# Expert sums moved to later blocks, and the overflow branch moved into the last block, in a two-layer encoder kernel

## The chip, the cores and the metric

The kernel runs on one core of a Trainium2 chip. The metric is the device time of one execution in microseconds; the kernel before has a median of 1400.67 us over three runs (1398.75 to 1402.1).

## The reference

Two layers on 512 tokens of width 1024, all in float32. Each layer is a mixer followed by a mixture of experts:

```python
x = x + hybrid_mixer(rmsnorm(x, norm_mix[l]), ...)        # attention + short convolution, one output projection
x = x + hierarchical_moe(rmsnorm(x, norm_ffn[l]), ...)    # 32 experts, 2 per token
...
return rmsnorm(x, norm_final)
# inside hierarchical_moe, for each block of token slots of one expert e:
y = (silu(xb @ w_gate[e]) * (xb @ w_up[e])) @ w_down[e]   # 1024 -> 512 -> 1024
```

A router chooses one of four groups and two of its eight experts for each token. The outputs of the two experts are weighted and added to the token's row. Each expert has 6 MB of weights, so one layer reads about 201 MB of them.

## The kernel before, in words

**Blocks.** The tokens of all experts are packed into 14 blocks of 128 slots (`BLOCKS`, L39). The experts are ranked by load; a block holds one expert of 128 slots, two of 64, or up to four of 32. A block therefore reads 12 weight tiles of 512 KB for each of its experts: 8 for gate and up, 4 for down. Blocks 2 and 12 have four experts, block 11 three, block 4 one, the others two. The first four experts are fixed (`STATIC`), the others are read by a number that the router has put into a register.

**One block** (`block`, L1223) runs on TensorE in written order (pinned): gate and up products in four quarters of the width (banks A, 64 to 128 matmul instructions), then a SiLU on ScalarE and a product on VectorE, four transposes, a copy, and the down products (banks C). Its result is weighted and split into a high and a low part (`yhi`, `ylo`, two places of the pool t4), with a 0/1 matrix `gm` (a place of the pool t2) that says which token each slot belongs to. The functions in `btw` are called between these steps, at quarter 0 to 3, behind the SiLU and product (`"a"`), behind the transposes (`"t"`) and ahead of the down products (`"y"`).

**Sums.** `combine(b, t)` (L1269) adds block b's result to token tile t: four matmuls into the banks D and F, which have one buffer each, and two additions on VectorE into x. Before, block 2 does the sums of blocks 0 and 1, block 3 those of block 2, and every later block those of the block before it, one token tile at a time. The last block does block 12's sums at quarter 0, at quarter 1, at "a" and at "t". Its own are done by `finish`, which begins some token tiles with x itself through an identity matmul (`begin`, L1280, two tiles in layer 0 and three in layer 1, called at "y").

**Gathers.** For the first three blocks the token rows are gathered straight from x (`gather1`); for the later ones from a high and a low part of x that block 2 writes (`parts`, `all_parts`), one or two blocks ahead (`gather`, four steps, banks B with two buffers). `rows_of` and `slots` bring each slot's token number, scale and gate; they need a table that VectorE makes in block 0.

**Loads.** All weight tiles of the kernel stand in one list in the order of use. SP issues them in that order, and the program asks for the next whenever a tile has been used:

```python
def pump(most=10 ** 6):
    while most and todo and mem["held"] < N4 - mem["keep"] and todo[-1][3] <= mem["routed"]:
```

The pool t4 has 42 places (`N4`); `mem["keep"]` of them are kept for results, gathered rows, one-hot matrices and the parts of x. It is 8 from block 1, 17 from the middle of block 2 (`KEEP_PARTS`), 15 from block 3 (`KEEP_MOE`), 21 in block 12 and 28 in the mixer (`KEEP_MIX`). The next layer's mixer weights stand behind the experts in the same list. A load also waits until the place it gets is really free.

**Overflow.** If an expert has more tokens than its slots, `spill` (L1046) does the rest in a loop under a condition (L1055). With these inputs the condition is false, and each engine only passes the branch. It stands ahead of block 13, with the last three down tiles of that block behind it in SP's order.

VectorE, ScalarE and GpSimdE are put in order by a planner in the expert blocks; TensorE and SP follow the program. L173 is the wrapper through which pinned instructions are recorded, so most of TensorE's rows carry that line.

Of the kernel before, what the change touches and what calls it, by code (L numbers as in the profile page):

```python
# [20 lines left out]
NT = S // P  # L21
ND = D // P
DEPTH = 2
# [45 lines left out]
GROUPS = [(0, 1), (2,), (3, 4), (5, 6), (7, 8), (9, 10), (11, 12), (13,)]  # L69
GROUP_OF = {b: j for j, g in enumerate(GROUPS) for b in g}  # L70
WHOLE = 3
MAXB = 32
NROW = 3 + 2 * E

# [84 lines left out]
R_ATT, R_CNV, R_W, R_F, R_L = 0, 4, 8, 20, 28  # L159
N4 = 42  # L160
N2 = 6
KEEP_MIX, KEEP_OUT, KEEP_ROUTE, KEEP_FIRST, KEEP_SECOND, KEEP_PARTS, KEEP_MOE = 28, 27, 5, 6, 8, 17, 15


class Engine:
# [11 lines left out]
def trunk(ctx, tc, x_d, norm_mix, w_in, attn_sink, conv_w, norm_attn_out, norm_conv_out, w_out,  # L177
# [25 lines left out]

    todo = []
    live = {}
    mem = {"held": 0, "keep": KEEP_MIX, "routed": -1}
    expert_of = {}

    def rows(w, n):
# [43 lines left out]

    perm = {}

    def pump(most=10 ** 6):
        while most and todo and mem["held"] < N4 - mem["keep"] and todo[-1][3] <= mem["routed"]:
            key, shape, src, _ = todo.pop()
            if isinstance(src, tuple):
                w, l, o, k0, k1 = src  # L260
                if o < STATIC:
                    src = w[l, o][k0:k1]
                else:
                    src = w[l][bass.ds(expert(l, o), 1), k0:k1, :].rearrange("o p f -> (o p) f")
                if len(shape) == 3:
                    src = src.rearrange("(p i) c -> p i c", i=2)
            t = t4(shape)
            nc.sync.dma_start(t, src)
            live[key] = t
            mem["held"] += 1  # L270
            most -= 1
# [652 lines left out]
    def order(l, q):  # L924

        kc, kr = q["kc"], q["kr"]
        a0 = _cols["rank"][0]
        sc = small("sc", [E, 8])
        V.tensor_copy(sc[:, 0:1], kc[:E, 0:1])
        above = small("above", [E, E], BF16)  # L930
        V.tensor_scalar(above, kr[:E], sc[:, 0:1], None, op0=OP.is_lt)
        rp = ps("B", (P, E))
        T.matmul(rp, onesb[:E], above, start=True, stop=True)

        mt = small("mt", [E, E])
        V.tensor_scalar(mt, rp[:E], cst[:E, a0:a0 + 1], None, op0=OP.is_equal)
        pf = small("pf", [E, E])
        V.tensor_tensor(pf, mt, iota[:E, :E], op=OP.mult)
        V.tensor_reduce(sc[:, 1:2], pf, axis=AX.X, op=OP.add)
        pm = small("perm", [E, 1], I32, bufs=2)  # L940
        V.tensor_copy(pm, sc[:, 1:2])
        perm[l] = pm
        mem["routed"] = l
        q.update(sc=sc, mt=mt)
# [189 lines left out]
    def moe(l, before):  # L1134
# [4 lines left out]
        def onehot(j):  # L1139

            b, w = GROUPS[j][0], len(GROUPS[j]) * P
            sq = small("sq", [P, 2, NT], bufs=2)
            GP.tensor_scalar(sq, q["v"][:, 16:18, :], -float(b * P), None, op0=OP.add)
            oh = t4([P, NT, 2 * P], F32R)
            io = iota[:, :w]
            for t in range(NT):
                V.tensor_scalar(oh[:, t, :w], io, sq[:, 0, t:t + 1], None, op0=OP.is_equal)  # L1147
                V.scalar_tensor_tensor(oh[:, t, :w], io, sq[:, 1, t:t + 1], f(oh[:, t, :w]), op0=OP.is_equal, op1=OP.add)
            ohq[j] = oh

        def gather1(b, c0, c1):

            if c0 == 0:
                hg[b] = t4([P, ND, P])
            j = GROUP_OF[b]
            s = (b - GROUPS[j][0]) * P
            for c in range(c0, c1, 2):
                p = ps("B", (P, 2, P))
                for cc in range(2):
                    for t in range(NT):  # L1160
                        T.matmul(p[:, cc], chunk(t, c + cc), f(ohq[j][:, t, s:s + P]), start=t == 0, stop=t == NT - 1)
                for cc in range(2):
                    A.activation(hg[b][:, c + cc], p[:, cc], AF.Copy, scale=g_ffn[:, c + cc:c + cc + 1])
# [37 lines left out]
        def rows_of(j):  # L1201
            w = len(GROUPS[j]) * P
            p = ps("B", (P, 2 * P))
            for t in range(NT):
                T.matmul(p[:NROW, :w], st["tab"][:, t], ohq[j][:, t, :w], start=t == 0, stop=t == NT - 1)
            st["rows"] = t2([NROW, 2 * P])
            A.activation(st["rows"][:, :w], p[:NROW, :w], AF.Copy)

        def slots(j):

            m = len(GROUPS[j])
            p = ps("B", (P, 2, 2 + E))
            for n in range(m):
                T.matmul(p[:, n], st["rows"][:, n * P:(n + 1) * P], C("sel")[:NROW], start=True, stop=True)
            g = small("tg", [P, 2, 3], bufs=4)
            V.tensor_copy(g[:, :m, :2], p[:, :m, :2])
            for n, b in enumerate(GROUPS[j]):
                tg[b] = g[:, n]
                for o in range(FIRST[b], FIRST[b] + len(BLOCKS[b])):
                    for s, w in tiles_of(OFF[o], SLOTS[o]):  # L1220
                        V.tensor_copy(g[s:s + w, n, 2:3], p[s:s + w, n, 2 + o:3 + o])
# [47 lines left out]
        def combine(b, t, tags="DF"):  # L1269
            yhi, ylo, gm = yy[b]  # L1270
            for n in range(2):
                s = slice(n * 512, (n + 1) * 512)
                p = ps(tags[n])
                T.matmul(p, gm[:, t * P:(t + 1) * P], yhi[:, s], start=True, stop=False)
                T.matmul(p, gm[:, t * P:(t + 1) * P], ylo[:, s], start=False, stop=True)
                V.tensor_add(x[:, t, s], x[:, t, s], p)  # L1276
# [3 lines left out]
        def begin(t):  # L1280

            sums[t] = [ps(tag) for tag in BANKS[l][t]]
            for n in range(2):
                T.matmul(sums[t][n], ident, x[:, t, n * 512:(n + 1) * 512], start=True, stop=False)
# [24 lines left out]

        def first():  # L1310

            rows_of(0)
            gather1(1, 0, 2)
            slots(0)

        def both(*what):
            return lambda: [fn() for fn in what]
# [6 lines left out]
        for b in range(NBLK):  # L1324
            if b == 5:
                nbb = past(q)
            if b == 6:
                et, ni = places(q, nbb)
            if b == 8:
                over = et, nc.values_load(  # L1330
                    ni[0:1, 0:1], min_val=0, max_val=MAXB,
                    skip_runtime_bounds_check_because="an expert's slots are 32 at least: fewer blocks than experts")
            c = [lambda t=t: combine(b - 1, t) for t in range(NT)]
            j = GROUP_OF[b] + 1
            if b == 0:
                btw = {0: lambda: order(l, q), 1: rest, 3: first, "a": lambda: gather1(1, 2, ND)}
            elif b == 1:
                mem["keep"] = KEEP_SECOND
                btw = {1: lambda: onehot(1), "a": both(lambda: rows_of(1), lambda: gather1(2, 0, 4)),
                       "t": both(lambda: slots(1), lambda: gather1(2, 4, ND))}  # L1340
            elif b == 2:
                c = [lambda t=t: (combine(0, t), combine(1, t)) for t in range(NT)]
                ga = [lambda k=k: gather(j, k) for k in range(0, ND, 2)]
                btw = {1: lambda: onehot(j), 2: all_parts, "a": both(lambda: rows_of(j), ga[0], c[0], ga[1], c[1]),
                       "t": both(ga[2], c[2], lambda: slots(j), ga[3], c[3])}
            elif b == NBLK - 1:
                btw = {0: c[0], 1: c[1], "a": c[2], "t": c[3]}
            elif b % 2:
                mem["keep"] = KEEP_MOE
                ga = [lambda k=k: gather(j, k) for k in (0, 2)]  # L1350
                btw = {1: lambda: onehot(j), "a": both(c[0], ga[0], c[1]), "t": both(c[2], ga[1], c[3])}
            else:
                ga = [lambda k=k: gather(j, k) for k in (4, 6)]
                btw = {"a": both(lambda: rows_of(j), c[0], ga[0], c[1]), "t": both(c[2], lambda: slots(j), ga[1], c[3])}
            pin(*((T,) if b < PIN_MOE else ()))
            if b == NBLK - 2:
                mem["keep"] = KEEP_MOE + 6
            if b == NBLK - 1:
                mem["keep"] = KEEP_MIX if l < DEPTH - 1 else KEEP_MOE
                if overflow:  # L1360
                    spill(l, q, *over)
                btw["y"] = lambda: [begin(t) for t in range(AHEAD[l])]
            block(b, btw)
        pin()
        return lambda t: finish(t) if l == DEPTH - 1 or t < AHEAD[l] else combine(NBLK - 1, t, BANKS[l][t])

    def nothing(t):
# [49 lines left out]
```

## Time and profile before

| | |
|---|---|
| runs, median (lowest to highest) | 1400.67 us (1398.75 to 1402.1) |
| profiled execution, its own time | 1399.71 us |
| its span, granted TensorE clock | 1397.9 us, 0.996 |
| TensorE busy | 1334.8 us (95%) |
| VectorE, ScalarE, GpSimdE busy | 607.0, 374.5, 118.9 us |
| read from HBM | 436 MB, 313 GB/s on the mean |

The span runs from the first to the last instruction; the execution's own time is 1.8 us more. The expert blocks of layer 0 run from about 230 to 697 us and those of layer 1 from about 921 to 1385 us. A busy TensorE is not one at its peak, because the ends of matmuls are modelled; what it waited for is in the views of waits.

### The profile page before, as it was taken

The page shows a single profiled execution, that of the slowest core. Times are in us where ns is not written, and L with a number is a line of the kernel's source. Part 1 is how long each engine was busy: PE and PEld are TensorE (multiplying, and loading weights), DVE is VectorE, ACT ScalarE, POOL GpSimd, SP SyncE. Part 2 cuts the span into 40 slices and gives each one's busy share as a digit, 9 for nine tenths or more (in the row PEclk, how much of TensorE's full clock was granted, in tenths as well). Part 3 has the DMA queues.
Part 4 walks back from the last instruction along what each step waited for, and adds up shares of the span by engine and source line. Part 5 has one row for each costly group of instructions (what it writes and reads, how often), then busy time and mean ns, then how long its engine had stood idle before and what let it go on. Part 6 is the DMA issues. An engine that isn't in the chain of part 4 may idle for free. (4 is left out here: it accounts for less than half of the span.)

```text
span 1397.9 us, 21902 instructions
## 1 busy us (share of the span) xinstructions
PE 1334.8 (95%) x7783; PEld 774.0 (55%) x7783; DVE 607.0 (43%) x1483; ACT 374.5 (27%) x816; POOL 118.9 (9%) x130
## 2 busy tenths in 40 slices
PE   5999999999999999999989999999999999999897
PEld 4888786545554444433368887865445444454143
DVE  4788845224244322312267888451442332333032
ACT  4556631221111111101155666222211111111012
POOL 2101440000000000000040014300000000000000
PEclk9999999999999999999999999999999999999999
DMA  8521368899999999999881224698999999999995
GB/s 268 170 76 61 116 247 300 347 375 355 419 385 390 419 418 419 418 419 419 331 265 46 76 63 149 256 342 334 382 383 418 360 418 419 418 419 419 419 418 222
DMA packets 161106, 439.61 MB, mean 314 GB/s; under 512 B 19368, under 2 KB 56416, under 8 KB 160992
## 3 DMA queue, kind: packets, MB, share of 16 engines
q1 hardware_dynamic: 160992, 438.16, 81.1%
q8 instruction: 63, 1.03, 0.3%
q14 instruction: 51, 0.42, 0.1%
HBM read 436.00 MB, written 2.10 MB: 313 GB/s over the span
## 5 line engine op out<-in xcount | busy, mean ns | idle before, releaser
L173 PE MATMUL A<-t,t 128*32 128x512 f32 (+3 forms) x3724 | 719.2, 526 | 16.9 <-DMA t<-in_w_expert_gate_dram 4.2
L173 PEld LDWEIGHTS A<-t,t 128*32 128x32 f32 (+2 forms) x3724 | 343.1, 144 | 351.0 <-issue 232.0
L173 PE MATMUL C<-t,t 128*32 128x512 f32 (+4 forms) x1384 | 233.6, 568 | 3.1 <-DMA t<-in_w_expert_down_dram 1.6
L173 PEld LDWEIGHTS C<-t,t 128*32 128x32 f32 (+2 forms) x1384 | 84.6, 128 | 136.8 <-issue 112.9
L390 DVE SCALAR_TENSOR_TENSOR t<-C,tg,t 128x512 fp32r<-128x512 f32 x56 | 41.5, 749 | 202.5 <-ACT t L389 200.7
L1245 DVE SCALAR_TENSOR_TENSOR t<-A,tg,t 128x512 f32<-128x512 f32 x28 | 21.0, 751 | 237.2 <-PE A L173 233.6
L173 PE MATMUL B<-t,t 128*128 128x256 f32 (+3 forms) x836 | 113.4, 285 | 7.2 <-DVE t L1170 4.7
L173 PEld LDWEIGHTS B<-t,t 128*128 128x128 f32 (+1 forms) x836 | 105.0, 188 | 24.3 <-DVE t L1170 7.6
L1276 DVE TENSOR_TENSOR x<-x,D 128x512 f32<-128x512 f32 x104 | 71.1, 684 | 92.0 <-PE D L173 91.6
L173 PE MATMUL D<-t,t 128*128 128x512 f32 (+1 forms) x374 | 99.8, 366 | 5.7 <-DVE t L387 2.9
L1244 ACT ACTIVATE t<-A,tg 128x512 f32<-128x512 f32 x28 | 19.2, 687 | 319.0 <-PE A L173 319.0
L389 ACT ACTIVATE t<-C,tg 128x512 fp32r<-128x512 f32 x56 | 37.8, 686 | 208.6 <-PE C L173 208.4
L173 POOL TENSOR_TENSOR t<-t,t 128x512 f32<-128x512 f32 (+1 forms) x34 | 63.8, 1880 | 234.0 <-PE A L173 122.1
L173 PE MATMUL B<-cst,t 128*128 128x128 f32 (+1 forms) x396 | 60.7, 281 | 20.2 <-DVE t L173 19.0
L1185 ACT ACTIVATE t<-B,gf 128x256 f32<-128x256 f32 (+1 forms) x96 | 38.6, 454 | 144.4 <-PE B L173 138.0
L173 PEld LDWEIGHTS D<-t,t 128*128 128x128 f32 x374 | 53.8, 179 | 32.5 <-issue 8.1
L173 PE MATMUL F<-t,t 128*128 128x512 f32 x214 | 71.3, 413 | 0.2
L1276 DVE TENSOR_TENSOR x<-x,F 128x512 f32<-128x512 f32 x104 | 70.7, 680 | 0.3 <-PE F L173 0.3
L173 PEld LDWEIGHTS B<-cst,t 128*128 128x128 f32 (+1 forms) x396 | 49.8, 153 | 32.3 <-issue 11.1
L173 PEld LDWEIGHTS F<-t,t 128*128 128x128 f32 x214 | 38.2, 190 | 17.1 <-DVE x L1276 9.1
L386 ACT ACTIVATE t<-t 128x1024 fp32r<-128x1024 f32 x44 | 46.1, 1057 | 0.2
L1147 DVE TENSOR_SCALAR t<-cst,sq 128x256 fp32r<-128x256 f32 (+1 forms) x64 | 17.2, 332 | 65.2 <-PE A L173 53.3
(250 smaller groups left out, 1019.1 us busy)
## 6 DMA issues: line engine op xcount, KB each, us to landing
t<-in_w_expert_gate_dram SPq DMA_DIRECT2D x256, 512.0 KB, 9.8
t<-in_w_expert_up_dram SPq DMA_DIRECT2D x256, 512.0 KB, 9.8
t<-in_w_expert_down_dram SPq DMA_DIRECT2D x256, 512.0 KB, 9.8
t<-in_w_in_dram SPq DMA_DIRECT2D x36, 512.0 KB, 6.3
t<-in_w_out_dram SPq DMA_DIRECT2D x16, 512.0 KB, 3.6
x<-in_x_dram SPq DMA_DIRECT2D x4, 512.0 KB
out_dram<-t SPq DMA_DIRECT2D x3, 512.0 KB, 2.6
t<-in_norm_mix_dram SPq DMA_DIRECT2D x2, 512.0 KB
```

Of the source, the lines that this page charges most:

```text
L173: return (lambda *args, **kw: self.tc.keep_in_program_order(fn(*args, **kw))) if self.pinned else fn
L386: A.activation(hi, src, AF.Copy)
L389: A.activation(hi, src, AF.Copy, scale=scale)
L390: V.scalar_tensor_tensor(lo, src, scale, f(hi), op0=OP.mult, op1=OP.subtract)
L1147: V.tensor_scalar(oh[:, t, :w], io, sq[:, 0, t:t + 1], None, op0=OP.is_equal)
L1185: A.activation(hg[b][c // 4][:, c % 4 + cc, :w], p[:, cc, :w], AF.Copy, scale=g_ffn[:, c + cc:c + cc + 1])
L1244: A.activation(a, pg, AF.Silu, scale=rs)
L1245: V.scalar_tensor_tensor(a, pu, rs, a, op0=OP.mult, op1=OP.mult)
L1276: V.tensor_add(x[:, t, s], x[:, t, s], p)
```

## The change

Block 0's sums are done in block 3, those of blocks 1 and 2 in block 4, those of 3 and 4 in block 5, and from block 6 on each block does those of the block before it, as it did. The last block does all four token tiles' sums of block 12 at quarters 0 and 1. The overflow branch moves from ahead of block 13 into it, to "a"; `begin` is called at "t". The places kept are 18 from block 2 and 20 in blocks 3 and 4; the last block keeps 15, and the mixer's tiles alone still obey 28 (`room`). In block 0 the first gather steps are called ahead of `rows_of` and `slots`.

```diff
+SUMS = {3: [0], 4: [1, 2], 5: [3, 4]}
...
-KEEP_PARTS, KEEP_MOE = 17, 15
+KEEP_PARTS, KEEP_LATE, KEEP_MOE = 18, 20, 15
...
+    def room(key):
+        return max(mem["keep"], KEEP_MIX) if key[0] in ("gm", "in", "rope", "mask", "out") and mem["experts"] else mem["keep"]
...
         def first():
+            gather1(1, 0, 2)
             rows_of(0)
-            gather1(1, 0, 2)
+            gather1(1, 2, 4)
             slots(0)
...
-            c = [lambda t=t: combine(b - 1, t) for t in range(NT)]
+            late = SUMS.get(b, [b - 1])
+            c = [lambda t=t: [combine(n, t) for n in late] for t in range(NT)]
...
             elif b == 2:
-                c = [lambda t=t: (combine(0, t), combine(1, t)) for t in range(NT)]
                 ga = [lambda k=k: gather(j, k) for k in range(0, ND, 2)]
-                btw = {1: lambda: onehot(j), 2: all_parts, "a": both(lambda: rows_of(j), ga[0], c[0], ga[1], c[1]),
-                       "t": both(ga[2], c[2], lambda: slots(j), ga[3], c[3])}
+                btw = {1: lambda: onehot(j), 2: all_parts, "a": both(lambda: rows_of(j), ga[0], ga[1]),
+                       "t": both(ga[2], lambda: slots(j), ga[3])}
             elif b == NBLK - 1:
-                btw = {0: c[0], 1: c[1], "a": c[2], "t": c[3]}
+                mem["keep"] = KEEP_MOE
+                btw = {0: both(c[0], c[1]), 1: both(c[2], c[3]), "a": lambda: spill(l, q, *over),
+                       "t": lambda: [begin(t) for t in range(AHEAD[l])]}
             elif b % 2:
-                mem["keep"] = KEEP_MOE
+                mem["keep"] = KEEP_LATE if b == 3 else KEEP_MOE
...
-            if b == NBLK - 1:
-                mem["keep"] = KEEP_MIX if l < DEPTH - 1 else KEEP_MOE
-                if overflow:
-                    spill(l, q, *over)
-                btw["y"] = lambda: [begin(t) for t in range(AHEAD[l])]
             block(b, btw)
```

## Rows read from the trace of the kernel before

**Rows 1.** Stretches of layer 0: length, busy time by engine, clock, DMA share, GB/s.

```profile
293.70:339.30 45.60, 42.33 (x302) 22.39 (x300) 20.92 (x36) 10.61 (x17) 0.23 (x1) 0.93 0.92 359
...
394.00:442.00 48.00, 48.00 (x295) 20.16 (x293) 17.42 (x47) 6.29 (x11) 0.23 (x1) 1.00 0.98 374
442.00:600.00 158.00, 158.00 (x1116) 76.64 (x1112) 53.47 (x113) 24.68 (x48) 0.23 (x1) 1.00 1.03 418
...
680.00:692.00 12.00, 11.74 (x44) 4.74 (x42) 3.53 (x6) 0.60 (x1) 0.00 (x0) 1.00 0.54 191
```

**Rows 2.** Waits of TensorE, 229.7 to 600 us: total, times, longest.

```profile
PE B L173 <- DVE t L1199: 1.2, 1, 1.2
```

**Rows 3.** Waits of TensorE, 600 to 660 us.

```profile
PE A L173 <- DMA t<-in_w_expert_gate_dram: 2.1, 9, 0.5
```

**Rows 4.** Waits of the SP queue in block 2, 293.7 to 339.3 us.

```profile
SPq L268 <- PE B L173: 9.0, 2, 8.6
```

**Rows 5.** Waits of the SP queue, 394 to 442 us.

```profile
SPq L268 <- PE A L173: 9.7, 11, 2.7
SPq L268 <- PE F L173: 6.2, 1, 6.2
```

**Rows 6.** Timeline of TensorE in block 2 of layer 1: start, us, instruction.

```profile
1004.03 0.63 PE L173 MATMUL D<-t,t 128*128 128x512 f32 x2
...
1005.45 0.73 PE L173 MATMUL D<-t,t 128*128 128x512 f32 x2 [0.32 <-DVE x L1276]
...
1006.61 2.07 PE L173 MATMUL B<-t,t 128*128 128x256 f32 x16
```

**Rows 7.** Costliest groups of the page: the gathers' evacuation.

```profile
L1185 ACT ACTIVATE t<-B,gf 128x256 f32<-128x256 f32 (+1 forms) x96 | 38.6, 454 | 144.4 <-PE B L173 138.0
```

**Rows 8.** Timeline of TensorE in blocks 3 and 4 of layer 1.

```profile
1028.05 13.95 PE L173 MATMUL A<-t,t 128*64 128x512 f32 x64
...
1071.70 0.63 PE L173 MATMUL D<-t,t 128*128 128x512 f32 x2
...
1072.62 2.08 PE L173 MATMUL B<-t,t 128*128 128x256 f32 x16
```

**Rows 9.** Timeline of TensorE in block 0 of layer 0.

```profile
246.08 0.69 PE L173 MATMUL B<-t,t 128*67 128x256 f32 x4 [1.24 <-DVE t L1199]
```

**Rows 10.** Timeline of TensorE in the last block, layers 0 and 1.

```profile
661.79 4.21 PE L173 MATMUL A<-t,t 128*64 128x512 f32 x16 [0.82 <-ACTq L1055]
...
681.49 0.73 PE L173 MATMUL D<-t,t 128*128 128x512 f32 x2
...
682.52 0.61 PE L173 MATMUL B<-cst,t 128*128 128x128 f32 x4
...
684.66 1.12 PE L173 MATMUL D<-x,cst 128*128 128x512 f32 x2 [0.26 <-DVE x L1276]
...
688.29 6.26 PE L173 MATMUL C<-t,t 128*64 128x512 f32 x26
694.78 1.93 PE L173 MATMUL C<-t,t 128*64 128x512 f32 x6 [0.23 <-DMA t<-in_w_expert_down_dram]
...
1377.91 7.09 PE L173 MATMUL C<-t,t 128*64 128x512 f32 x32
```

**Rows 11.** The branch's line, layer 0: count, ns, first and last start.

```profile
L1055 SPq EVENT_SEMAPHORE  x9: 17/17/17, 676.6 to 686.3; - x9
L1055 PEldq COMPARE_BRANCH  x1: 353/353/353, 659.1 to 659.1; - x1
L1055 PEldq EVENT_SEMAPHORE  x1: 51/51/51, 661.0 to 661.0; - x1
...
L1055 SPq COMPARE_BRANCH  x1: 50/50/50, 676.4 to 676.4; - x1
```

**Rows 12.** Timeline of the SP queue at the end of layer 0.

```profile
676.03 11.82 SPq L268 DMA_DIRECT2D t<-in_w_expert_down_dram  x3
...
693.33 28.85 SPq L268 DMA_DIRECT2D t<-in_w_in_dram  x17
```

More of the change, by code (lines that the diff above doesn't have):

```diff
@@ L161 @@
 N2 = 6
-KEEP_MIX, KEEP_OUT, KEEP_ROUTE, KEEP_FIRST, KEEP_SECOND, KEEP_PARTS, KEEP_MOE = 28, 27, 5, 6, 8, 17, 15
+KEEP_MIX, KEEP_OUT, KEEP_ROUTE, KEEP_FIRST, KEEP_SECOND, KEEP_PARTS, KEEP_LATE, KEEP_MOE = 28, 27, 5, 6, 8, 18, 20, 15
 class Engine:
@@ L205, in trunk @@
     live = {}
-    mem = {"held": 0, "keep": KEEP_MIX, "routed": -1}
+    mem = {"held": 0, "keep": KEEP_MIX, "routed": -1, "experts": False}
     expert_of = {}
@@ L254, in trunk @@
     perm = {}
+    def room(key):
+        return max(mem["keep"], KEEP_MIX) if key[0] in ("gm", "in", "rope", "mask", "out") and mem["experts"] else mem["keep"]
     def pump(most=10 ** 6):
-        while most and todo and mem["held"] < N4 - mem["keep"] and todo[-1][3] <= mem["routed"]:
+        while most and todo and mem["held"] < N4 - room(todo[-1][0]) and todo[-1][3] <= mem["routed"]:
             key, shape, src, _ = todo.pop()
@@ L1332, in moe @@
                     skip_runtime_bounds_check_because="an expert's slots are 32 at least: fewer blocks than experts")
-            c = [lambda t=t: combine(b - 1, t) for t in range(NT)]
+            late = SUMS.get(b, [b - 1])
+            c = [lambda t=t: [combine(n, t) for n in late] for t in range(NT)]
             j = GROUP_OF[b] + 1
             if b == 0:
-                btw = {0: lambda: order(l, q), 1: rest, 3: first, "a": lambda: gather1(1, 2, ND)}
+                mem["experts"] = True
+                btw = {0: lambda: order(l, q), 1: rest, 3: first, "a": lambda: gather1(1, 4, ND)}
             elif b == 1:
@@ L1341, in moe @@
             elif b == 2:
-                c = [lambda t=t: (combine(0, t), combine(1, t)) for t in range(NT)]
                 ga = [lambda k=k: gather(j, k) for k in range(0, ND, 2)]
-                btw = {1: lambda: onehot(j), 2: all_parts, "a": both(lambda: rows_of(j), ga[0], c[0], ga[1], c[1]),
-                       "t": both(ga[2], c[2], lambda: slots(j), ga[3], c[3])}
+                btw = {1: lambda: onehot(j), 2: all_parts, "a": both(lambda: rows_of(j), ga[0], ga[1]),
+                       "t": both(ga[2], lambda: slots(j), ga[3])}
             elif b == NBLK - 1:
-                btw = {0: c[0], 1: c[1], "a": c[2], "t": c[3]}
+                mem["keep"] = KEEP_MOE
+                btw = {0: both(c[0], c[1]), 1: both(c[2], c[3]), "a": lambda: spill(l, q, *over),
+                       "t": lambda: [begin(t) for t in range(AHEAD[l])]}
+                if not overflow:
+                    del btw["a"]
             elif b % 2:
-                mem["keep"] = KEEP_MOE
+                mem["keep"] = KEEP_LATE if b == 3 else KEEP_MOE
                 ga = [lambda k=k: gather(j, k) for k in (0, 2)]
@@ L1357, in moe @@
                 mem["keep"] = KEEP_MOE + 6
-            if b == NBLK - 1:
-                mem["keep"] = KEEP_MIX if l < DEPTH - 1 else KEEP_MOE
-                if overflow:
-                    spill(l, q, *over)
-                btw["y"] = lambda: [begin(t) for t in range(AHEAD[l])]
             block(b, btw)
         pin()
+        mem["keep"] = KEEP_MIX if l < DEPTH - 1 else KEEP_MOE
+        mem["experts"] = False
         return lambda t: finish(t) if l == DEPTH - 1 or t < AHEAD[l] else combine(NBLK - 1, t, BANKS[l][t])
```

## The prediction

> **What bounds the kernel now.** I read the page's slices first: in both layers the transfers run near 420 GB/s through most of the expert blocks and far below it in the mixers, so the expert stage is where this change can act. Then a table by stretches of layer 0 [rows 1]. Block 2 (293.7 to 339.3 us) moved 359 GB/s, blocks 5 and 6 (394 to 442) 374, and from 442 to 600 it is 418 with TensorE busy throughout. After that the waits of TensorE: up to 600 us it waits on no transfer at all, only on other engines; from 600 to 660 it waits on expert weights [rows 2, 3]. So the stage has two halves. First TensorE sets the pace and the transfers stop for lack of free buffers; then the blocks of three and four experts come, transfers set the pace, and the stage ends when the last tile has landed. A tile is 512 KB, 1.25 us at 418 GB/s.
>
> The queue that issues the loads (SP) shows what ties the halves together [rows 4, 5]: in block 2 it stood 8.6 us on one gather's matmul, in blocks 5 and 6 on TensorE's expert products (9.7 us) and 6.2 us on one sum's matmul (F). All of these are buffers given back late by TensorE. From 442 us on nothing stops it but its own pace. Therefore the end of the stage moves by what TensorE's time moves up to block 6, not by how the idle transfer time is spread before that: an early gap that is filled only runs sooner into the same limit of buffers.
>
> **The change part by part.** Layers repeat each other, so I price one and say where they differ.
>
> *Sums leave block 2.* There two sums of one token tile stand back to back. The first starts at 1004.03 and the gather behind the second at 1006.61: 2.58 us, with a 0.32 us wait for VectorE to have emptied the same bank D [rows 6]. Four pairs are 10.3 us. They also cover bank waits of the gathers: without them a gather that needs the bank of the one two places back waits for two evacuations of 0.454 us [rows 7] with only four short matmuls (about 0.5) in between, twice, 2 x 0.4 to 0.5 = about 1.0. Net -9.3 us of TensorE time in block 2; nothing is late instead, for block 3's first ten weight tiles have been issued before the gap.
>
> *Sums arrive in blocks 3, 4 and 5.* Block 3 does block 0's sums in place of block 2's, same count: 0. Blocks 4 and 5 do two blocks' sums in place of one, and again back to back on the banks D and F. A lone sum costs 0.92 us to the next matmul (1071.70 to 1072.62) [rows 8]; I take four at 4.1, since one of them follows the transposes and meets a bank not yet emptied. Four pairs are 10.3 as above. So +6.2 each, +12.4 together. This is dearer than what block 2 gives, because eight pairs now meet the busy bank where four did. Bounds: if VectorE's additions overlapped fully a pair would be 2 x 0.92 and each block +3.3; if every addition had also to wait for other VectorE work, I add half a us to a pair, +8.2.
>
> *Fewer weight tiles held* (18 places kept for other tiles in place of 17 in block 2, 20 in place of 15 in blocks 3 and 4). In block 4 the queue may be 5 tiles shorter, 6.3 us of transfer. Block 5's first 22 of 24 tiles still fit before its products begin, so TensorE does not starve: 0 on its own account. What it takes is reserve, which has to be refilled in block 5.
>
> *First block.* TensorE stood 1.24 us for the table before rows_of [rows 2, 9]; the first gather, 16 matmuls, needs only the one-hot tile and now fills it. Some of it returns as bank waits of 0.25 each between the reordered gathers. I take -1.0 (ends 0 and -1.6).
>
> TensorE's time up to block 6 is therefore -1.0 - 9.3 + 12.4 = +2.1 us a layer. In layer 0 the granted clock of block 2 is 0.93 on the mean [rows 1], and part of that stretch lies behind waits for the high and low parts of x; those waits stay, and what runs at the lower level is then the gathers in place of the sums. I leave that out of the sum and in the range. I pass the whole +2.1 on to the stream of loads. The ends: -1.3 (if transfers run without a break from block 5's products on, they are one tile ahead at 442 us) and +4.6 (the full 2.1 and two tiles late, 2 x 1.25, since block 5 now holds two blocks' results of two places each).
>
> *Last block, sums in its own waits.* Its expert products stand from 661.79 to 681.49, 19.7 us, of which 64 matmuls are 13.95, as in block 3 [rows 8], and two sums 2.2; the rest, 3.5, is waiting for weights, and 0.82 stand ahead of it for the branch [rows 10]. Two more sums and their pair waits are 2.9 us more work (two pairs of 2.58 in place of two sums) against 4.3 of waiting. Not all of the waiting lies behind them: I take the end of the products 0.4 later in layer 0 and, where the same stretch is 0.6 shorter (an estimate), 0.9 later in layer 1. Between the products and the first matmul of the next sums there were 3.17 us (681.49 to 684.66). Of these the chain product, transposes keeps 1.03 + 0.61 (681.49 to 682.52 and the transposes); the two sums and a 0.26 wait for VectorE go: -1.5. The branch joins this chain.
>
> *The branch.* Before, each engine passed it between blocks 12 and 13. SP went in at 676.4 and came out at 686.3, having waited for its loads in flight, and the last three down tiles were issued only then [rows 11, 12]; 680 to 692 us moved 191 GB/s [rows 1]. TensorE's down products started at 688.29 and ended at 694.78 + 1.93 = 696.7 where layer 1's took 7.09 without a break [rows 10]: 1.3 us lost on those tiles. Now the three are issued ahead of the branch and follow at 1.25 each, done near 687, while their products begin at 687: the 1.3 goes. In its new place the branch stands ahead of the transposes, which need VectorE to have passed it. VectorE's own passage is not in the rows; TensorE's took from 659.1 to 661.0, part of it finishing its matmuls [rows 11]. Bounds 0 and 1.9; I take 0.3, for the engines that had nothing left to finish needed only their compare (50 ns on SP). Six loads of the next layer now go out before the branch and SP waits for them too; the others follow at about 695 us (687 and six times 1.25), where before the second w_in tile and those behind it began at 693.3 [rows 12]. 0, covered by the norm and transposes that the next layer begins with.
>
> Tail: layer 0: +0.4 - 1.5 + 0.3 - 1.3 = -2.1; layer 1 has no stall on down tiles: +0.9 - 1.5 + 0.3 = -0.3.
>
> **Sum.** 2 x 2.1 - 2.1 - 0.3 = +1.8 us on the profiled execution's 1399.71 (span 1397.9 and 1.8 around it), 1401.5. That execution lies 1.0 below the median of the runs shown, 1400.67, so the median becomes 1402.5. A measurement of this kernel tells 0.2%, 2.8 us, from no change: my forecast is no change that can be told, on the slower side.
>
> **The rivals.**
>
> *The stream keeps what block 2 loses.* 45.6 us at 359 in place of 418 GB/s are 6.5 us of transfer in layer 0 [rows 1]. For it: the 8.6 us wait is SP's longest in that block, and it does go. Against it: the limit is met again by 442 us, and at block 5's products the stream now stands at 22 tiles of that block and not 27. Without any break from there it gains 1.3 a layer; with the tail at its better end (branch 0, products not late: -2.8 and -1.5) the time is 1400.67 - 2.6 - 4.3 = 1393.8; with half of that, 1397. Chance 0.24. The Trainium skill has the rule that speaks for it (Perfetto Trace Analysis, Identifying the Most-Contended Engine: take the engine with the highest use, transfers by their bandwidth, and improve that first); by it the 6.5 us of layer 0 would come back in full. No run here shows that yet; the trace shows the limit returning.
>
> *Slower: results held two blocks on starve SP in block 5.* Place: 405 to 425 us and the like in layer 1, where SP already waited 6.2 us on a sum's F matmul [rows 5]. With two blocks' results in the buffers until the last pair of block 5, that wait begins earlier and ends later. It decides once SP stands longer than the tiles in flight last, about 10 us, since the page has a load land 9.8 us after its issue. Price: two tiles more a layer, 2.1 + 2.5 each: 1400.67 + 9.2 - 2.4 = 1407.5. Chance 0.20.
>
> *Slower: the branch on the chain.* 1.9 us exposed in each layer in place of 0.3, and SP's wait for the six loads of the next layer holding the rest back: 1402.5 + 3.2 = 1405.7, more if layer 1's first products then wait. For it: it now lies on the one chain that ends each layer. Against it: TensorE's 1.9 includes the end of its matmuls, which has to be waited for anyway. Chance 0.10.
>
> **How the numbers follow.** Forecast 0.46 (1399 to 1404.5 with the stage at +1 to +3 a layer), the stream 0.24, starved SP 0.20, branch 0.10. Faster by over 0.2% (below 1397.9): nearly all of the stream's rival, 0.22, and 0.02 of the forecast's edge: 0.24. Slower by over 0.2% (above 1403.5): 0.18 of the starved queue, 0.08 of the branch, 0.05 of the forecast's upper edge: 0.31. Same 0.45. The range for 8 times in 10 is 1396 to 1408: below it is the better half of the stream's rival, above it both layers at the upper end. The forecast's own range is 1399 to 1404.5.
>
> **What would show it.** TensorE's sums gone from block 2, the next block starting some 10 us sooner; in blocks 4 and 5 four pairs of about 2.6 us, and block 6 starting about 2 us later than before. SP's 8.6 us wait on a gather gone, a longer one on a sum's F matmul in block 5; the table's rate near 418 in block 2 and lower than 374 in blocks 5 and 6. In layer 0's last block no idle transfers between 680 and 687 us and no wait of the down products; their start about 1 us sooner after the last weights. Wrong would be: block 6 starting sooner than before, a rate of 400 or more from 394 to 442, or transposes of the last block over 1 us behind the product.

## The result, and the profile after

The changed kernel took 1407.65 us on the median (1405.83 to 1408.32, 4 runs), the kernel before 1399.71 (1398.24 to 1402.1, 4 runs) on the same chip: ratio 1.0053, 95% interval 1.0038 to 1.0068. It is slower by some 7 us, more than the 0.2% that can be told from no change. The forecast was 1402.5 us and no change that can be told; slower than that had a chance of 0.31. The result lies above the forecast's own range (1399 to 1404.5), 0.35 us inside the wide one (1396 to 1408), and at the time of a rival (1407.5). The profiled execution has a span of 1406.5 us, 8.6 more than before, and granted clock 0.993 against 0.996.

Line numbers shift: L173 is now L175, L268 L274, L1055 L1061, L1170 L1176, L1276 L1282. First the stretches of layer 0 after (length, busy time by engine, clock, DMA share, GB/s), against [rows 1]:

```profile
293.70:339.30 45.60, 41.90 (x314) 19.79 (x312) 14.76 (x30) 11.56 (x19) 0.46 (x2) 0.96 1.02 407
394.00:442.00 48.00, 46.60 (x266) 20.38 (x268) 22.57 (x55) 5.49 (x10) 0.23 (x1) 1.00 0.87 329
442.00:600.00 158.00, 158.00 (x1108) 71.98 (x1100) 49.74 (x106) 23.51 (x44) 0.23 (x1) 1.00 1.03 417
680.00:692.00 12.00, 10.47 (x44) 3.84 (x40) 1.87 (x4) 1.28 (x2) 0.00 (x0) 1.00 1.03 416
```

Block 2's stretch gained 48 GB/s and 394 to 442 us lost 45, where the queue stopped. The waits of SP, first in block 2 (against [rows 4]), then from 394 to 442 us (against [rows 5]): the 8.6 us on a gather have become 2.1, the 6.2 us on a sum's F matmul 10.4.

```profile
SPq L274 <- PE B L175: 2.5, 2, 2.1
```

```profile
SPq L274 <- PE F L175: 11.8, 2, 10.4
SPq L274 <- PE A L175: 9.4, 10, 2.6
```

A pair of sums in block 4 (start, us, instruction) is 2.57 us (374.28 to 376.85) with the same 0.33 wait for VectorE as in [rows 6]:

```profile
374.28 0.63 PE L175 MATMUL D<-t,t 128*128 128x512 f32 x2
...
375.68 0.73 PE L175 MATMUL D<-t,t 128*128 128x512 f32 x2 [0.33 <-DVE x L1282]
...
376.85 2.07 PE L175 MATMUL B<-t,t 128*128 128x256 f32 x16
```

Block 2 of layer 1, without sums, shows what they had covered: waits for an evacuation (0.49) and for VectorE's slots (0.77).

```profile
1005.60 4.67 PE L175 MATMUL B<-t,t 128*128 128x256 f32 x25 [0.63 <-DVE t L1176]
1010.11 0.60 PE L175 MATMUL B<-cst,t 128*128 128x128 f32 x4
1011.20 2.18 PE L175 MATMUL B<-t,t 128*128 128x256 f32 x16 [0.49 <-ACT t L1191]
1013.21 0.53 PE L175 MATMUL B<-cst,t 67*128 67x34 f32 x4
1014.52 2.15 PE L175 MATMUL B<-t,t 128*128 128x256 f32 x16 [0.77 <-DVE tg L1227]
```

From the transposes (1010.11) to the next gather are 1.09 us, from the slots' matmuls (1013.21) to theirs 1.31. In the kernel before, with sums ahead of each, they were 0.35 and 0.37:

```profile
1011.10 0.60 PE L173 MATMUL B<-cst,t 128*128 128x128 f32 x4
1011.45 2.16 PE L173 MATMUL B<-t,t 128*128 128x256 f32 x16
...
1016.02 0.53 PE L173 MATMUL B<-cst,t 67*128 67x34 f32 x4
1016.39 2.15 PE L173 MATMUL B<-t,t 128*128 128x256 f32 x16
```

The 25 gather matmuls at 1005.60 had a granted clock of 0.67 on the mean of their stretch, so they ran largely at the lower of the two levels, 1.2 GHz:

```profile
1005.00:1010.20 5.20, 4.60 (x26) 4.61 (x27) 0.54 (x1) 0.84 (x2) 0.00 (x0) 0.67 1.03 420
```

One thing is not in the program's order: in both layers 36 of block 8's 128 products (tiles 128*32) stand among block 7's sums.

```profile
479.87 0.63 PE L175 MATMUL D<-t,t 128*128 128x512 f32 x2
480.43 1.06 PE L175 MATMUL A<-t,t 128*32 128x512 f32 x6
481.42 0.73 PE L175 MATMUL F<-t,t 128*128 128x512 f32 x2
481.99 0.60 PE L175 MATMUL B<-cst,t 128*128 128x128 f32 x4
482.51 1.90 PE L175 MATMUL A<-t,t 128*32 128x512 f32 x10
...
489.05 1.92 PE L175 MATMUL A<-t,t 128*32 128x512 f32 x14
```

The last block of layer 0, against [rows 10], and the branch's rows on VectorE, against [rows 11] (count, ns, first and last start):

```profile
668.78 1.93 PE L175 MATMUL A<-t,t 128*64 128x512 f32 x6 [0.22 <-DMA t<-in_w_expert_up_dram]
...
679.78 7.09 PE L175 MATMUL A<-t,t 128*64 128x512 f32 x32
688.39 0.63 PE L175 MATMUL B<-cst,t 128*128 128x128 f32 x4 [1.53 <-DVEq L1061]
...
692.38 7.09 PE L175 MATMUL C<-t,t 128*64 128x512 f32 x32
```

```profile
L1061 DVEq COMPARE_BRANCH  x1: 72/72/72, 687.6 to 687.6; - x1
L1061 DVEq EVENT_SEMAPHORE  x1: 21/21/21, 688.2 to 688.2; - x1
```

The down products now run without a break (7.09), and the transposes stand 1.52 behind the products' end (679.78 + 7.09 = 686.87) against 1.03 before (in layer 1 there are 1.08 after). Behind VectorE's product, which ends at 687.73, they stand 0.66, under the 1 us that the prediction names as a sign of being wrong; behind TensorE's products it was over 1 us before, too.

Taken from the timelines at each boundary, the 8.6 us of span come out so (changed less before, us):

| stretch | forecast a layer | layer 0 | layer 1 |
|---|---|---|---|
| ahead of block 0: first mixer; second mixer | 0 | +1.24 | +0.64 |
| block 0 | -1.0 | -0.74 | -0.74 |
| block 2 | -9.3 | -9.2 | -7.1 |
| blocks 4 and 5 | +12.4 | +12.9 | +12.9 |
| start of block 0 to start of block 6 (sum) | +2.1 | +2.96 | +5.04 |
| start of block 6 to end of block 12 | 0 | +0.50 | +0.59 |
| last block, to the end of its down products | -2.1; -0.3 | -1.94 | -0.45 |

### The profile page after: what moved, and what is told of

The parts are those of the page before. It is cut to its first block, busy times and chain, and to the rows that moved or that the text cites. A ratio compares the mean times of both kernels' runs of the same rounds, so it can differ in the third digit from the quotient of the medians.

```text
span 1406.5 us, 21931 instructions
## 1 busy us (share of the span) xinstructions
PE 1340.6 (95%) x7783; PEld 774.8 (55%) x7783; DVE 608.9 (43%) x1483; ACT 374.0 (27%) x816; POOL 118.8 (8%) x130
## 3 DMA queue, kind: packets, MB, share of 16 engines
q8 instruction: 63, 1.03, 0.3%
## 5 line engine op out<-in xcount | busy, mean ns | idle before, releaser
L175 PE MATMUL A<-t,t 128*32 128x512 f32 (+3 forms) x3724 | 720.7, 527 | 13.9 <-DMA t<-in_w_expert_up_dram 4.0
L175 PEld LDWEIGHTS A<-t,t 128*32 128x32 f32 (+2 forms) x3724 | 343.5, 145 | 344.2 <-issue 240.0
L175 PE MATMUL C<-t,t 128*32 128x512 f32 (+4 forms) x1384 | 232.1, 567 | 3.0 <-ACT t L1256 1.5
L175 PEld LDWEIGHTS C<-t,t 128*32 128x32 f32 (+2 forms) x1384 | 84.5, 128 | 134.8 <-issue 112.9
L175 PE MATMUL B<-t,t 128*128 128x256 f32 (+3 forms) x836 | 115.0, 289 | 7.4 <-DVE t L1176 4.9
L175 PEld LDWEIGHTS B<-t,t 128*128 128x128 f32 (+1 forms) x836 | 106.7, 191 | 23.1 <-DVE t L1176 7.8
L175 PE MATMUL D<-t,t 128*128 128x512 f32 (+1 forms) x374 | 99.7, 365 | 9.9 <-DVE x L1282 6.4
L1282 DVE TENSOR_TENSOR x<-x,D 128x512 f32<-128x512 f32 x104 | 71.3, 685 | 83.9 <-PE D L175 83.5
L175 POOL TENSOR_TENSOR t<-t,t 128x512 f32<-128x512 f32 (+1 forms) x34 | 63.8, 1881 | 236.2 <-PE A L175 124.3
L175 PE MATMUL B<-cst,t 128*128 128x128 f32 (+1 forms) x396 | 61.6, 284 | 21.7 <-DVE t L175 18.0
L175 PEld LDWEIGHTS D<-t,t 128*128 128x128 f32 x374 | 53.3, 177 | 40.6 <-issue 13.2
L1282 DVE TENSOR_TENSOR x<-x,F 128x512 f32<-128x512 f32 x104 | 70.8, 680 | 7.5 <-PE F L175 7.5
L175 PE MATMUL F<-t,t 128*128 128x512 f32 x214 | 72.0, 416 | 0.2
L175 PEld LDWEIGHTS B<-cst,t 128*128 128x128 f32 (+1 forms) x396 | 50.4, 154 | 34.7 <-issue 12.7
L175 PEld LDWEIGHTS F<-t,t 128*128 128x128 f32 x214 | 36.7, 188 | 23.1 <-DVE x L1282 14.2
L1149 POOL TENSOR_SCALAR sq<-rv 128x8 f32<-128x8 f32 x16 | 3.9, 248 | 492.0 <-DVE t L1154 456.9
```

The lines of the kernel that those rows point to most:

```text
L175: return (lambda *args, **kw: self.tc.keep_in_program_order(fn(*args, **kw))) if self.pinned else fn
```

## The experiments

Theory *TensorE*: the time goes as the start of block 6 goes; TensorE's work up to there frees the buffers, and behind it the loads run without a break to the end. Rivals: *places* (results held two blocks, and the higher reserves, leave too few places for weights), *branch*, and *order* (block 8's stray products). Ratios are to the kernel before, with 95% intervals, from 5 to 11 runs of each kernel. Diffs are to the change, unless said otherwise; e7, e8, e9, e11 and e12 also have e4's accumulation and e6's order. TensorE's marks, in us:

| run | layer 0: block 0 starts, block 6 starts, block 12 ends | layer 1 |
|---|---|---|
| before | 229.69, 428.65, 660.98 | 920.57, 1117.38, 1349.51 |
| after | 230.93, 432.85, 665.68 | 923.97, 1125.82, 1358.54 |
| e1_last | 230.86, 428.81, 661.15 | 919.70, 1117.88, 1349.89 |
| e2_sums | 229.06, 431.19, 663.31 | 922.76, 1123.85, 1356.84 |
| e3_keep | 230.85, 434.24, 666.07 | 924.54, 1127.94, 1360.04 |
| e4_joint | 230.81, 426.49, 660.37 | 917.67, 1113.00, 1345.82 |
| e5_first | 230.75, 427.89, 660.01 | 920.89, 1118.26, 1350.24 |
| e6_order | 230.71, 432.51, 664.83 | 923.24, 1125.15, 1357.16 |
| e7_lag2 | 230.90, 422.02, 656.37 | 914.53, 1105.68, 1339.95 |
| e8_lag3 | 230.80, 418.33, 655.33 | 915.43, 1104.20, 1341.37 |
| e9_joint2 | 230.72, 423.95, 656.03 | 914.45, 1109.19, 1341.09 |
| e10_cap | 230.89, 429.13, 660.73 | 920.64, 1118.82, 1350.88 |
| e11_back | 231.30, 422.22, 656.30 | 913.95, 1104.90, 1339.65 |
| e12_lag2k | 232.53, 425.15, 658.67 | 916.61, 1110.79, 1344.60 |

**e1_last: the last block alone.**

```diff
-SUMS = {3: [0], 4: [1, 2], 5: [3, 4]}
+SUMS = {2: [0, 1]}
...
-KEEP_PARTS, KEEP_LATE, KEEP_MOE = 18, 20, 15
+KEEP_PARTS, KEEP_LATE, KEEP_MOE = 17, 15, 15
```

(and `first` as before)

> The kernel before with the last block's part alone: its sums at the first two quarters, the branch ahead of the transposes behind the loads, the next sums begun behind them. Theory TensorE (the time was lost because TensorE reaches block 6 later, and the loads only carry that to the end): block 6 starts where it does before (428.65 and 1117.38, within 0.5), and from block 12's last matmul to the end of block 13's down products layer 0 is 1.9 us shorter and layer 1 0.4, as between the two kernels' traces; the time is 2.3 us below the kernel before (ratio 0.998 to 0.999). Rival branch (the branch on the chain costs 1.9 us a layer): no gain, 0 to +1.5 us.

Measured 0.9989 (0.9980 to 0.9998), -1.5 us. Block 6 starts within 0.5 of before, so the gain is the last block's. The branch costs about 0.5 in layer 0, where the wait below is 1.52 and 1.03 stood before, and 0.2 in layer 1 (1.23 for 1.05): near the forecast's 0.3, and not 1.9.

```profile
683.84 0.63 PE L175 MATMUL B<-cst,t 128*128 128x128 f32 x4 [1.52 <-DVEq L1061]
```

**e2_sums: the later sums and the reserves alone** (`first`, `room` and the last block as before).

> The kernel before with the sums taken two blocks on and the two reserves (18 and 20 places) alone; first and last block as before. Theory TensorE: block 6 starts 3.7 us later than before in layer 0 (-9.2 + 6.3 + 6.6) and another 5.8 later in layer 1, counted from block 0; 9 to 10.5 us slower than before (ratio 1.0065 to 1.0075). Rival branch: the deferral costs only the +2.1 a layer of the forecast, 4 us (1.003), and the rest of the loss sits in the last block.

Measured 1.0074 (1.0061 to 1.0088), +10.4 us: more than the whole loss sits here. With e1's and e5's factors the product is 1.0074 x 0.9989 x 0.9988 = 1.0051, the 1.0053 of the change.

**e5_first: block 0's order alone** (the diff is to before; the gather at "a" begins with column block 4).

```diff
+            gather1(1, 0, 2)
             rows_of(0)
-            gather1(1, 0, 2)
+            gather1(1, 2, 4)
```

> The kernel before with the first block's new order alone (the first gather ahead of rows_of). Theory TensorE, by the trace of the changed kernel: block 0 is 0.74 us shorter (263.90 - 230.93 in place of 263.40 - 229.69), the stream's end follows, 1.5 us over both layers, ratio 0.9985 to 0.9995. Rival: what block 0 gains is waited off in block 2 on the parts of x, 0, ratio 1.000.

Measured 0.9988 (0.9979 to 0.9997), -1.7 us, as theory TensorE has it.

**e3_keep: the change with the reserves of before.**

```diff
-KEEP_PARTS, KEEP_LATE, KEEP_MOE = 18, 20, 15
+KEEP_PARTS, KEEP_LATE, KEEP_MOE = 17, 15, 15
```

> The changed kernel with the reserves of before (17 places in block 2, 15 in blocks 3 and 4) in place of 18 and 20. Theory TensorE: block 6 starts where it does in the changed kernel, within 0.5 us a layer, and the time is the same within 1 us (1.0053 of before). Rival places (the loads are late because fewer weight tiles may be held while results wait): SP's 10.4 us wait on a sum's F matmul in block 5 shrinks by the 5 tiles that it may run ahead (about 6 us), and the time falls by 2.5 us a layer or more, to 1402.5 or below.

Measured 1.0063 (1.0050 to 1.0077). Not faster: rival places falls as far as the reserves go. TensorE's part of the expectation missed too, block 6 starts 1.5 later in each layer. SP ran further ahead and stood longer (from 400 to 445 us):

```profile
SPq L274 <- PE F L175: 13.6, 2, 12.2
```

and a gather of block 4 waited for VectorE's slots, which nothing in the changed kernel does there (TensorE's waits, 360 to 400 us):

```profile
PE B L175 <- DVE tg L1227: 1.3, 1, 1.3
```

**e10_cap: the kernel before with reserves 18 and 20** (the diff is to before).

```diff
-                mem["keep"] = KEEP_MOE
+                mem["keep"] = KEEP_LATE if b == 3 else KEEP_MOE
```

> The kernel before with the higher reserves alone (18 places in place of 17 in block 2, 20 in place of 15 in blocks 3 and 4); sums as before. Theory TensorE: SP runs less far ahead in blocks 3 and 4 and then waits less in block 5; block 6 starts as before and the time is the same within 1 us. Rival places: one to two tiles a layer are lost, 2.5 to 5 us slower (1.002 to 1.0035).

Measured 0.9999 (0.9989 to 1.0009). The reserve that the forecast costed at nothing costs nothing. SP's wait on a sum in block 5 only shrinks, from the 6.2 of [rows 5]:

```profile
SPq L268 <- PE F L173: 5.7, 2, 5.4
```

**e6_order: block 8's products kept behind block 7.** The register load of the overflow count stands between the two blocks. The edit ties this load alone to block 7's last matmul; if the products then stay behind block 7, it was the load that the planner had taken early, with the products behind it.

```diff
+                bb = nc.cur_bb.bb
+                n0 = len(bb.instructions)
+                tail = [i for i in bb.instructions if i.engine == mybir.EngineType.PE][-1]
                 over = et, nc.values_load(
...
+                for i in bb.instructions[n0:]:
+                    if i.engine == mybir.EngineType.PE:
+                        tc.add_manual_dep(i, tail.name, mybir.DependencyInfo(
+                            mybir.DependencyClass.NoSync, mybir.DependencyReason.DATA), reason="behind block 7")
```

> The changed kernel with block 8's first products kept behind block 7's last matmul; in the changed kernel's trace 36 of them stand among block 7's sums, and TensorE needs 62.28 us from block 7 to block 9 in place of 59.58. Theory TensorE (the stream's end is set by block 6): block 9 starts 2.7 us sooner, but from 442 to 520 us the loads had lost only 3 GB/s, about 0.6 us, so the time falls by 0.5 to 1.2 us over both layers. Rival order: all of 2.7 us a layer comes back, 5.4 us, 1402.

Measured 1.0044 (1.0030 to 1.0058), some 1.3 us less than the change, though the two intervals overlap. The products stand together again:

```profile
492.04 13.94 PE L175 MATMUL A<-t,t 128*32 128x512 f32 x128
```

From block 6 to the end of block 12 there are 232.32 and 232.01 us, as before (232.33, 232.13), where the change had 232.83 and 232.72. So the stray order cost the change at most the 0.5 or 0.6 a layer behind block 6, and most of TensorE's 2.7 us was hidden. That it is the cause of the 0.5 is not shown: the same order stands in e2 and e3, which have 231.8 to 232.1 in three layers and 233.0 in the fourth.

**e4_joint: the change, with a pair's two sums in one accumulation.**

```diff
...
+                for i, b in enumerate(late):
+                    yhi, ylo, gm = yy[b]
+                    T.matmul(p, gm[:, t * P:(t + 1) * P], yhi[:, s], start=i == 0, stop=False)
+                    T.matmul(p, gm[:, t * P:(t + 1) * P], ylo[:, s], start=False, stop=i == len(late) - 1)
+                V.tensor_add(x[:, t, s], x[:, t, s], p)
```

> The changed kernel, with the two sums of a pair accumulated in one bank and added to x once per half (8 matmuls, 2 additions in place of 8 and 4), so that the wait of 0.32 for VectorE in each pair has no cause; block 8's products then stand behind block 7's as before. Theory TensorE: a pair costs about 2.1 in place of 2.5, eight pairs 3.2 a layer; block 6 starts 3.2 us a layer sooner than in the changed kernel, and the time falls by 6.4 + about 1 for block 8's order, to 1400 to 1401, level with before. Rival elsewhere (the wait only moves to the next gather or to VectorE): at most 1 us a layer, 1405 to 1406.

Measured 0.9963 (0.9951 to 0.9975), 12.6 us below the change by ratio, more than expected. A pair is 1.82 (374.05 to 375.87), twice a lone sum's 0.92, not 2.1:

```profile
374.05 1.08 PE L175 MATMUL D<-t,t 128*128 128x512 f32 x4
374.96 1.07 PE L175 MATMUL F<-t,t 128*128 128x512 f32 x4
375.87 2.08 PE L175 MATMUL B<-t,t 128*128 128x256 f32 x16
```

Eight pairs of 0.75 less are 6.0 a layer; block 6 starts 6.24 and 6.52 sooner after block 0 than in the change. Theory TensorE holds: the deferral itself stayed, the wait in each pair went, and the loss with it. But not all of TensorE's gain reached the end of block 12: from block 6 on there are 233.9 and 232.8 us, 1.6 and 0.7 more than before, and though TensorE is ahead of before, 394 to 442 us run at 366 GB/s, below its 374:

```profile
394.00:442.00 48.00, 48.00 (x304) 22.36 (x301) 18.25 (x47) 5.19 (x10) 0.23 (x1) 1.00 0.95 366
```

**e9_joint2: the change without the deferral, block 2's pairs accumulated.**

```diff
-SUMS = {3: [0], 4: [1, 2], 5: [3, 4]}
+SUMS = {2: [0, 1]}
```

(reserves 17 and 15)

> The kernel before with the first and last blocks of the change, and block 2's pairs in one accumulation each (sums not taken later, reserves as before). Theory TensorE: block 6 starts 4 times 0.4 + 0.7 = 2.3 us a layer sooner than before, last blocks 2.3 shorter in all: 6 to 7 us below before (1393 to 1394.5, ratio 0.995). Rival elsewhere: only the last blocks' 2, 1398.

Measured 0.9935 (0.9923 to 0.9947), -9.1 us, more than expected, since a pair saves 0.75 and not 0.4. Block 6 starts 4.7 us sooner than before in layer 0 (a part of it is the clock of block 2, 1.00 here and 0.93 there), block 12 ends 4.95 sooner, and 394 to 442 us run at 391 GB/s:

```profile
394.00:442.00 48.00, 48.00 (x312) 22.24 (x313) 19.50 (x51) 6.60 (x13) 0.23 (x1) 1.00 0.99 391
```

Against e4, which differs from it by the deferral and its reserves, e9 is 4 us faster. From the start of block 0 to that of block 6 it gains 0.6 in layer 1, where both had the lower clock; behind block 6 it needs 232.1 and 231.9 us where e4 needed 233.9 and 232.8. So the deferral costs something behind block 6 too once TensorE is no longer late, as rival places has it; that it is the places held, and not the later place of the sums, is not shown.

**e7_lag2 and e8_lag3: every block's sums later by one or two blocks, nothing doubled ahead of block 12** (reserves 17, and 18 to 19; e7 has block 0's sums in block 2).

```diff
-SUMS = {3: [0], 4: [1, 2], 5: [3, 4]}
+SUMS = {2: [0], **{b: [b - 2] for b in range(3, 12)}, 12: [10, 11]}
```

> Block 2 takes block 0's sums alone, each block from 3 to 11 those of two blocks before it, block 12 those of blocks 10 and 11 (in one accumulation), block 13 block 12's; reserve of 17 places from block 2 on; the first and the last block as in the changed kernel; block 8 in order. Theory TensorE: no pair stands ahead of block 12, so block 6 starts some 5 us (block 2's second sums) and 0.7 (first block) sooner than before in each layer, the loads from 394 to 442 us run above 374 GB/s, and the time is 10 to 13 us below the kernel before (1387 to 1390, ratio 0.991 to 0.993). Rival places: with results held over two blocks in every block SP stands on their F matmuls as in the changed kernel, and the loads gain nothing: 1398 to 1400.

```diff
+SUMS = {**{b: [b - 3] for b in range(3, 12)}, 12: [9, 10], 13: [11, 12]}
```

> As the one before, one block later: no sums in block 2, each block from 3 to 11 takes those of three blocks before it, block 12 those of 9 and 10, block 13 those of 11 and 12; reserve 18 and 19. Theory TensorE: block 6 starts about 9 us sooner a layer than before; the idle transfer time that can be won from 294 to 442 us is 6.5 + 5.1 in layer 0 and some 9 in layer 1, so the gain is 7 to 9 us a layer, less up to 2 for the doubled sums of the last block: 1382 to 1388. Rival places: six places held by results (7.5 us of loads) give the gain back, 1398 or more.

e7: 0.9918 (0.9904 to 0.9931), -11.5 us, as theory TensorE has it. e8: 0.9965 (0.9953 to 0.9978), -4.9, at 1396.0 us far from its 1382 to 1388 and nearer to rival places' 1398. Here the rule ends: from block 6 to the end of block 12 e7 needs 234.3 us and e8 237.0, against 232.1. That results held longer are the cause is likely, since e7's loads run at 378 GB/s from 394 to 442 us, under e9's 391, but no run has TensorE as far ahead without holding them. e8's last block is also longer by 2.2 us in layer 1 (8.14 ahead of before at block 12's end, 5.9 at the end).

**e11_back and e12_lag2k: which places?** e11 catches up in block 6 (`6: [4, 5]`, reserve 15 from block 7); e12 is e7 with reserves 17 and 15.

> Sums as in the run with a lag of two blocks up to block 5, then block 6 takes blocks 4 and 5 (one accumulation) and every later block the one before it, so that results are held two blocks only from block 3 to block 6; the last block as in the changed kernel. Block 6 starts as early as in the lag-two run (some 6.6 and 5 us sooner, counted from block 0). Theory TensorE alone: the stream's end is the same as there, the same time, ratio 0.9918. Theory TensorE with places (up to some 5 us the loads follow TensorE; beyond that the two places more that results hold are missing, since there the stream's end came 4.6 us sooner for 6.6 of TensorE in layer 0 and 2.8 for 5.0 in layer 1): the two places given back after block 6 let the loads follow further, 1 to 2 us a layer better, ratio 0.989 to 0.9905.

> The lag-two kernel with the reserve of before (15 places from block 3 on) in place of 17. From block 6's start to the end of block 12 there were 232.1 us in nearly all runs, 234.3 in the lag-two run and 237.1 in the lag-three run: two and four places of 1.25 us. Theory reserve (the written reserve of 17 holds the loads two tiles back): 232.1 again, 2 us a layer less, 4 us in all, ratio 0.989. Theory places (the results themselves take two places more, and these are missing whatever the reserve says): 234 to 234.5 again, the same time, ratio 0.992.

e11: 0.9923 (0.9910 to 0.9937), the same as e7; from block 6 on 234.1 and 234.75. Places given back behind block 6 help nothing. e12: 0.9954 (0.9940 to 0.9967), 5 us worse than e7. Its 233.5 and 233.8 are neither 232.1 nor 234.3; most was lost ahead of block 6: blocks 4 and 5 take 3.05 us more than in e7 in both layers. Half of that is the same wait for VectorE's slots as in e3 (TensorE's waits, 360 to 395 us). The other half is the clock: the gather right behind that wait took 3.65 us, against 2.16 in e7, at a granted clock of 0.53.

```profile
PE B L175 <- DVE tg L1227: 1.4, 1, 1.4
```

```profile
383.76 3.65 PE L175 MATMUL B<-t,t 128*128 128x256 f32 x16 [1.41 <-DVE tg L1227]
```

```profile
383.70:387.30 3.60, 3.54 (x17) 3.57 (x18) 0.00 (x0) 0.00 (x0) 0.00 (x0) 0.53 1.02 418
```

Neither theory of the two foresaw that. In both kernels the weights were allowed places that results were about to need; that VectorE's writes then stood in front of the slots is likely, not shown.

## Why the prediction was right in the mechanism and wrong in a size

**What bounds the kernel: right.** TensorE waits for no transfer up to 600 us in the change either, and in before, e1, e2, e3, e5, e6, e9 and e10 block 12 ends 231.6 to 233.0 us after block 6 starts, 14 of these 16 times 231.8 to 232.4, while block 6 itself moves by over 5 us. Outside this list e4 has 233.9 and 232.8, and e7, e8, e11 and e12 have 233.5 to 237.2. An early gap filled in block 2 (407 GB/s) came back as a stop in block 5 (329). So the rival in which the stream keeps block 2's 6.5 us fell. By the Trainium skill (Perfetto Trace Analysis, Identifying the Most-Contended Engine) the engine of highest use, transfers by their bandwidth, is to be improved first. For block 2's transfers the traces do not bear that out: their rate rose, and by the 6.5 us layer 0 should have ended sooner, but it ended later (TensorE's work had grown meanwhile). What brought a gain was less work of TensorE, and the loads followed (e9).

**The size of the deferral: wrong, and this is the step that failed.** "TensorE's time up to block 6", in the sum +2.1 us a layer, should have been about +3.8. The profiled execution of before is a poor measure for it: between these marks it has 198.96 and 196.81 us, with a granted clock of 0.93 and 1.00 in block 2, where e1 and e10 have 197.95 to 198.24, with 0.96 in both layers. Against the mean of these, 198.1, the change's 201.92 and 201.85 (clock 0.95) are +3.8 a layer. By parts: block 2 is 36.4 after, and 44.5 to 44.9 in e1, e5 and e10, so -8.3 and not -9.3. The term that was mis-sized most is the 1.0 for the waits that the sums had covered: in the rows above there are 1.09 us in place of 0.35 and 1.31 in place of 0.37, 1.7 more in all. With the clock full on both sides block 2 goes from 43.48 (before, layer 1) to 34.87 us (e2, layer 1), -8.6, so the clock that I left "out of the sum and in the range" explains only some 0.3 of the miss: the lower level was met on both sides, and cost about 1.2 in e1, e5 and e10 and 1.5 in the change. Blocks 4 and 5 are +12.9 and not +12.4, block 0 -0.74 and not -1.0.

**Program order: an unforeseen cost.** I took TensorE to follow the program. Block 8's stray products cost 0.6 a layer at most.

**Reserve at nothing: right** (e10). **The last block: right**, -1.94 and -0.45 against -2.1 and -0.3, term by term in layer 0: products' end 0.7 later after block 12 (forecast 0.4), the chain from there to the down products 1.3 shorter (-1.5 + 0.3), the stall on down tiles gone (-1.3). Where 680 to 692 us moved 191 GB/s, 684.7 to 696.7, as far behind block 12, now move 396.

**The rival that had the time had, for this change, the wrong cause.** "Slower: results held two blocks on starve SP in block 5" gave 1407.5. Its sign came true, a 10.4 us wait on F in block 5, but its price of 2.5 a layer did not: the stretch behind block 6 grew by 0.6 at most, and not at all in e6, and with the pairs accumulated, results held just as long, the loss against before is gone (e4). In the change that wait tells that SP had run ahead, not that a transfer was late. The rival was not empty, though: e4 needs 0.9 to 1.8 us a layer more than e9 behind block 6, which held results may explain. That the range of 1396 to 1408 holds the measured time is luck: it reached so far for loads two tiles late in each layer, which did not come.

**The rest.** 1.24 us of the span stand ahead of block 0 and 0.64 in the second mixer; ten of the twelve experiments start block 0 between 230.7 and 231.3 us, so this is mostly an early profiled execution of before. Twice 3.8, up to 1.1 behind block 6 and -2.4 make +5.2 to +6.3; the ratio's interval is +5.3 to +9.5 us. What lies between that and the ratio's 7.4 is not accounted for.

## What to carry to other kernels

Where TensorE first sets the pace and loads later, price an edit by TensorE's time up to the point where the loads stop waiting, and check that mark in every trace; a better rate ahead of it is no gain in itself. Work that is doubled up on one bank should be accumulated there, with one addition behind it: that was worth 0.75 us a pair, and taking sums one block later, with none doubled ahead of block 12, gave the best kernel here (e7: 1389.6 us, 0.9918; e11 is level with it). Taking them later still was not free: e4 lost 4 us against e9, and e8 lost more than half of e7's gain. When work leaves a stage, list the waits that stood behind it before its time is booked as gained.

## What the hardware showed beside this

Products on 128*32 tiles are cheap only in a row: 128 of them take 13.94 us, 0.11 each, but 6 among sums took 1.06, 10 took 1.90 and 14 took 1.92, 0.14 to 0.19 each. And the same gathers behind much the same waits met different clocks: block 2 had a granted clock of 0.93 and 1.00 in the two layers of before, 0.96 in both of e1, e5 and e10, 0.95 in both of the change, and 0.95 and 1.00 in e2. In this block e2's two layers differ by 1.0 us and before's by 2.1, so a difference of that size between two traces can be the clock and not the edit; which level an execution gets no row here tells.
